# A two-layer hybrid trunk: scan rows loaded two chunks ahead, convolution steps spread over the pieces, output projections in quarters of 512 columns

## The chip, the cores and the metric

The kernel runs on one core of a Trainium2 chip. The metric is the device time of one execution in microseconds (us), the median of several runs. Five engines work side by side and wait for each other by semaphores: PE (TensorE, matrix products into PSUM), DVE (VectorE), ACT (ScalarE), POOL (GpSimd) and SP (SyncE, which here only issues transfers). Each engine takes its instructions in the order that was fixed when the kernel was built.

## The reference, cut to what matters

One sequence of 1024 tokens, width 1024, passes through two residual layers and a final norm.

```
u = rmsnorm(x)                                  # layer 0
z, xBC, dt, q, k, v, g = split(u @ w_in)
xBC = silu(causal_dwconv(xBC))                  # 4 taps; gives xs, B, C
y_a = rmsnorm((ssd_scan(xs, dt, A, B, C) + xs * D) * silu(z))   # 4 groups of 4 heads, chunks of 128
y_b = rmsnorm(diff_attention(q, k, v)) * silu(g)                # 8 heads
x = x + concat(y_a, y_b) @ w_out                # 2048 -> 1024
u = rmsnorm(x)                                  # layer 1
q, f, i, g = split(u @ w_in)
x = x + (rmsnorm(gated_linear_recurrence(q, f, i)) * silu(g)) @ w_out   # 16 heads, 2048 -> 1024
out = rmsnorm(x)
```

## The kernel before, in words

Every large product is made in three passes (hi*hi, hi*lo, lo*hi): each operand is split into a rounded part and a rest. `_wprep` does that for a block of weights of 1024 rows by 256 columns: two transfers into `w_raw` (two buffers), a cast on ACT (L132, `w_hi`) and a subtraction on DVE (L133, `w_lo`). `w_hi` and `w_lo` have two buffers each. `mm_cm` (L174) makes products of 512 columns with the weights stationary, `mm_tm` (L184) products of 256 columns with the activations stationary.

Tiles come from tags with a fixed number of buffers (`SLOTS`); whoever wants a buffer waits until its last user is done. Tags that matter here: `A` (11 buffers of 4 KB a partition), `V` (4), `G` (2), `wT`, `th`, `ey` and `cm` (1 each), `u` (16). PSUM has two banks of tag `pj`, two of `s1` and two double banks `big`. The builder orders the instructions of all engines by its own estimate of times, except PE's in the scan stage of layer 0, where the order is written out by `weave`.

**Start.** `norm_first` loads eight row tiles of x, scales each (L848, by a factor from DVE and POOL), transposes them and splits them into `u`. `setup_rows` loads small rows of parameters, which the first split needs too. The first block of weights is asked for after that.

**Scan stage.** For each of the four groups, `ssd_pieces` makes twelve pieces of 24 products for the next group: four for xs, four for B and C, four for the gate z. After the fourth and the eighth piece all convolution taps (L435) and their SiLU (L438, L439) follow at once. A gate piece leaves PSUM by `silu2`: a Tanh on ACT into `th` (L232), then DVE (L233) into an `A` tile. `weave` puts the scan of the present group between these pieces: `first(c)` of chunk c after piece 1.5 + 1.5c, `second(c)` two pieces later; in the last group, whose pieces are the attention's first ones, after 1.5 + c. `first` loads the rows of cumulated decays for four heads, spread over 128 partitions (`R`, L464), and makes the scores from them (L482, L484, L485). `second` makes the products, loads another spread copy of the decays for every two chunks (`ea`, L523, exponential L525), combines (L529, L530), and for every two chunks adds the skip (L537), gates (L540), squares into `th` (L542) and sums the squares on POOL (L544, L547).

**Output projections.** In both layers `out_proj` walks column blocks of 256. The first half of the contraction (8 tiles of `ya`) runs for both halves of the tokens and is added to x1. The second half (8 tiles of `yb`) has the halves of the tokens outside and the column blocks inside, so its weights are split twice; it ends with the sums of squares (L781) and `finish`: the next layer's norm and transposes, or the final scaling and the store (L998 to L1004). `load_y` brings two tiles at a time through `w_raw`, or one through `th` or `ey`, and splits them.

Of the kernel before, what the change touches and what calls it, by code (L numbers as in the profile page):

```python
# [19 lines left out]
P = 128  # L20
# [69 lines left out]
class Net:  # L90
# [23 lines left out]
    def _wprep(self, i):  # L114
# [4 lines left out]
        hi = self.t("w_hi", [P, KT, WB], F32R)  # L119
        lo = self.t("w_lo", [P, KT, WB], F32R)  # L120
        for q in range(2):
            raw = self.t("w_raw", [P, KT // 2, WB])
            k0 = q * (KT // 2)
            o = 0
            for c0, n in cols:
                nc.sync.dma_start(
                    raw[:, :, o:o + n],
                    src[row0 + k0 * P:row0 + (k0 + KT // 2) * P, c0:c0 + n].rearrange(
                        "(k p) n -> p k n", p=P))
                o += n  # L130
            hq, lq = hi[:, k0:k0 + KT // 2, :], lo[:, k0:k0 + KT // 2, :]
# [47 lines left out]
    def mm_tm(self, out, w, uh, ul, ks=range(KT)):  # L179
        nc = self.nc  # L180
        wh, wl = w
        for k in ks:
            for j, (uu, ww) in enumerate(((uh, wh), (uh, wl), (ul, wh))):
                nc.tensor.matmul(out, lhsT=uu[k], rhs=ww[:, k, :],  # L184
                                 start=(k == 0 and j == 0), stop=(k == KT - 1 and j == 2))
# [20 lines left out]
    def proj_v(self, u):  # L206
        vs = []
        run(self.v_pieces(u, vs))
        return self.v_of(vs)

# [202 lines left out]
def ssd_pieces(S, u, g, out):  # L413

    nc = S.nc

    def conv(w, cis):
        outs = [S.t("A", [P, L]) for _ in range(2)]
        rps = [S.t("V", [P, L]) for _ in range(2)]
        for hf in range(2):  # L420
            for mt in range(2):
# [7 lines left out]
                if not (hf and mt):  # L429
                    yield  # L430
        for mt in range(2):
            cv, rp, ci = outs[mt], rps[mt], cis[mt]
            for k in range(2, -1, -1):
                d = 3 - k
                nc.vector.scalar_tensor_tensor(cv[:, d:], rp[:, :L - d], S.convw[:, k, ci:ci + 1], cv[:, d:],  # L435
                                               op0=ALU.mult, op1=ALU.add)
            th = S.t("p1", [P, L])
            nc.scalar.activation(th, cv, AF.Tanh)  # L438
            nc.vector.scalar_tensor_tensor(cv, th, 1.0, cv, op0=ALU.add, op1=ALU.mult)  # L439
        out.extend(outs)  # L440
        yield

    yield from conv(S.wnext(), (2 * g, 2 * g + 1))
    if g == 0:
        dt_stage(S, u)
    yield from conv(S.wnext(), (8 + g, 12 + g))
    zg = []
    for _ in S.gate_pieces(u, "AA", zg):
        yield
# [3 lines left out]
def ssd_steps(S, g, tiles, ya, at, lag):  # L453
# [4 lines left out]
    X_, sts, eas = {}, {}, {}  # L458

    def first(c):  # L460
        x0, x1, Bt, Ct = tiles[:4]
        cs = slice(c * P, c * P + P)
        R = S.t(("G", "G", "wT")[(8 * g + c) % 3], [P, 4, P])
        nc.sync.dma_start(R, bc(S.acs_d[hs, cs].unsqueeze(0), [P, 4, P]))  # L464
# [15 lines left out]
        nc.vector.tensor_tensor(cb, pt[:, 384:512], S.triu, op=ALU.mult)  # L480
        for h in range(4):
# [4 lines left out]
        X_[c] = pk, R  # L486

    def second(c):
        Ct = tiles[3]
        cs = slice(c * P, c * P + P)  # L490
        pk, sc = X_[c]
# [26 lines left out]
        if c % 2 == 0:  # L518

            c2 = slice(c * P, (c + 2) * P)  # L520
            ea = S.t("ey", [P, 2, 256])
# [4 lines left out]
            eas[c // 2] = ea, S.t("o", [P, 2, 256])  # L526
        ea, tt = (z[:, :, (c % 2) * P:(c % 2) * P + P] for z in eas[c // 2])
# [5 lines left out]
        if c % 2 == 1:  # L533
            t = eas[c // 2][1]
# [6 lines left out]
            sq = S.t("th", [P, 2, 256])  # L541
# [147 lines left out]
def load_y(S, y_d, wcols, hf, k, tags):  # L689

    nc = S.nc
    n = len(tags)
    raw = S.t("w_raw" if n == 2 else (("th", "ey")[k % 2] if hf else "th"), [P, n, 512])
    nc.sync.dma_start(raw, y_d(k, n)[:, :, hf * 512:hf * 512 + 512].rearrange("b p t -> p b t"))
# [500 lines left out]
```

## Time and profile before

| | |
|---|---|
| median of 3 runs | 2238.65 us (2238.03 to 2240.89) |
| profiled execution | 2242.69 us, its span 2240.9 us |
| PE busy | 2178.8 us, 97% of the span |
| DVE, ACT, POOL busy | 1269.9, 832.2, 188.8 us |
| granted clock of TensorE, mean | 0.991 |
| PE in the chain that ended last, L174 and L184 | 24% and 19% |

The span runs from the first to the last instruction of the profiled execution. Busy time is time in which an engine had an instruction at work; PE's matmuls overlap, so its rate is read from the distance of their starts. The granted clock is 1.00 at 2.4 GHz and 0.50 at 1.2 GHz.

### The profile page before, as it was taken

How to read it: one execution, taken by the hardware profiler on the slowest of the kernel's cores; microseconds unless marked ns; L12 is line 12 of the kernel's file. 1: busy time of each engine (PE TensorE's matmuls, PEld its weight loads, DVE VectorE, ACT ScalarE, POOL GpSimd, SP SyncE). 2: the span in 40 equal slices, each digit the busy share in tenths (PEclk: the TensorE clock that was granted, in tenths of full speed). 3: DMA queues.
4: the chain of work that ended last, by engine and by line, in shares of the span. 5: the costliest groups of instructions: out<-in, count | busy, mean ns of one | idle time of the engine just before them, and what ended most of it. 6: DMA issues, size and time to landing. Idle time of an engine off the chain costs nothing.

```text
span 2240.9 us, 40897 instructions
## 1 busy us (share of the span) xinstructions
PE 2178.8 (97%) x16868; PEld 1920.3 (86%) x16868; DVE 1269.9 (57%) x2864; ACT 832.2 (37%) x1903; POOL 188.8 (8%) x216
## 2 busy tenths in 40 slices
PE   6998998899999999999999999999999999999998
PEld 5787776789898988999988989898989898989998
DVE  4765766565656556755453555555555555557444
ACT  4333333234444545644442323232323222324233
POOL 1001111110000000000010010101010101010000
PEclk9999999999999999999999999999999999999999
DMA  4322233332212221525331111111111111125333
GB/s 138 67 84 66 80 85 81 74 81 64 69 36 67 64 69 41 170 66 159 119 104 39 48 48 48 48 48 48 48 48 48 48 49 48 48 67 165 111 103 122
DMA packets 182256, 169.14 MB, mean 75 GB/s; under 512 B 10239, under 2 KB 163233, under 8 KB 182068
## 3 DMA queue, kind: packets, MB, share of 16 engines
q1 hardware_dynamic: 174564, 152.42, 23.1%
q0 software_dynamic: 3280, 9.90, 2.1%
q10 hardware_dynamic: 4224, 4.19, 0.6%
q8 instruction: 132, 2.16, 0.4%
q14 instruction: 56, 0.46, 0.1%
HBM read 132.66 MB, written 25.43 MB: 71 GB/s over the span
## 4 chain that ended last, share of the span: by engine, by line
PE 51%; DMA 1%; ACT 0%; DVE 0%; issue 0%; POOL 0%; POOLq 0%; ACTq 0%
PE pj L174 24%; PE pj L184 14%; PE big L184 5%; PE big L1051 2%; PE big L1139 1%; PE big L1141 1%; PE s L1128 1%; PE big L1093 1%; PE s L1155 1%; PE s L1122 1%; PE big L1087 0%; PE s L159 0%; DMA ey<-yb 0%; DMA th<-in_lvmask 0%; ACT w_hi L132 0%; DVE w_lo L133 0%
## 5 line engine op out<-in xcount | busy, mean ns | idle before, releaser
L174 PE MATMUL pj<-u,w_hi 128*128 128x512 f32 x3072 | 990.0, 400 | 31.3 <-DVE A L233 21.2
L174 PEld LDWEIGHTS pj<-u,w_hi 128*128 128x128 f32 x3072 | 573.4, 190 | 154.7 <-DVE A L233 23.0
L174 PE MATMUL pj<-u,w_lo 128*128 128x512 f32 x1536 | 607.9, 396 | 0.0
L184 PE MATMUL pj<-w_hi,u 128*128 128x256 f32 x2592 | 492.6, 286 | 1.0 <-DVE A L233 1.0
L184 PEld LDWEIGHTS pj<-w_hi,u 128*128 128x128 f32 x2592 | 409.9, 191 | 3.6 <-DVE A L233 1.4
L184 PE MATMUL pj<-w_lo,u 128*128 128x256 f32 x1296 | 368.3, 284 | 0.0
L174 PEld LDWEIGHTS pj<-u,w_lo 128*128 128x128 f32 x1536 | 291.8, 190 | 61.1 <-issue 0.2
L133 DVE TENSOR_TENSOR w_lo<-w_raw,w_hi 128x1024 fp32r<-128x1024 f32 x168 | 206.3, 1251 | 116.9 <-ACT w_hi L132 116.6
L184 PEld LDWEIGHTS pj<-w_lo,u 128*128 128x128 f32 x1296 | 247.8, 191 | 1.0
L132 ACT CAST w_hi<-w_raw 128x1024 fp32r<-128x1024 f32 x168 | 168.1, 1047 | 188.8 <-PE pj L174 107.6
L233 DVE SCALAR_TENSOR_TENSOR A<-th,pj 128x512 f32<-128x512 f32 x80 | 55.1, 689 | 140.9 <-ACT th L232 140.4
L232 ACT ACTIVATE th<-pj 128x512 f32<-128x512 f32 x96 | 57.2, 596 | 208.5 <-PE pj L174 190.8
L617 ACT ACTIVATE p<-p,mx 128x256 f32<-128x256 f32 (+7 forms) x128 | 98.5, 771 | 72.4 <-DVE mx L613 66.4
L148 POOL TENSOR_TENSOR ro<-rs_t,mhalf 128x4 f32<-128x4 f32 x48 | 52.8, 1100 | 682.4 <-DVE rs_t L147 489.1
L603 PE MATMUL big<-A 128*128 128x512 f32 (+3 forms) x384 | 90.3, 352 | 2.6 <-DMA A<-A 1.3
L968 POOL TENSOR_SCALAR A<-th,fN,fB 128x512 f32<-128x512 f32 x32 | 47.6, 1488 | 470.0 <-ACT th L965 470.0
L637 ACT COPY wT<-s 128x512 f32<-128x512 f32 (+2 forms) x96 | 45.8, 477 | 95.8 <-PE s L635 95.1
L639 PE MATMUL s<-V,wT 128*128 128x128 f32 x576 | 79.7, 275 | 0.6 <-ACT wT L637 0.6
L1035 DVE TENSOR_TENSOR A<-A,p 128x512 f32<-128x512 f32 x96 | 65.8, 686 | 23.5 <-PE big L1051 23.0
L639 PEld LDWEIGHTS s<-V,wT 128*128 128x128 f32 x576 | 74.4, 191 | 3.3 <-ACT wT L637 1.1
L1030 DVE TENSOR_TENSOR p<-p,p 128x512 f32<-128x512 f32 x96 | 66.2, 690 | 15.5 <-PE big L1087 6.2
L603 PEld LDWEIGHTS big<-A 128*128 128x128 f32 x384 | 64.5, 189 | 11.3 <-issue 2.3
(330 smaller groups left out, 2977.1 us busy)
## 6 DMA issues: line engine op xcount, KB each, us to landing
w_raw<-in_even_w_in SPq DMA_DIRECT2D x32, 512.0 KB, 4.7
w_raw<-in_odd_w_in SPq DMA_DIRECT2D x64, 256.0 KB, 3.3
w_raw<-in_odd_w_in SPq DMA_DIRECT2D x32, 512.0 KB, 3.9
w_raw<-in_even_w_in SPq DMA_DIRECT2D x48, 256.0 KB, 4.3
w_raw<-in_even_w_out SPq DMA_DIRECT2D x24, 512.0 KB, 4.4
w_raw<-in_odd_w_out SPq DMA_DIRECT2D x24, 512.0 KB, 4.6
A<-A POOLq DMA_DIRECT2D x32, 256.0 KB, 5.5
yo<-ey SPq DMA_DIRECT2D x32, 256.0 KB, 2.0
```

The lines of the kernel that those rows point to most:

```text
L132: nc.scalar.copy(hq, raw)
L133: nc.vector.tensor_tensor(lq, raw, hq.bitcast(F32), op=ALU.subtract)
L148: return nc.gpsimd.tensor_tensor(dst, t[:, :n], self.mhalf[:, :n], op=ALU.pow)
L174: nc.tensor.matmul(out, lhsT=ww[:, k, ms], rhs=uu[k][:, sl], start=(n == 0), stop=(n == 3 * KT - 1))
L184: nc.tensor.matmul(out, lhsT=uu[k], rhs=ww[:, k, :], start=(k == 0 and j == 0), stop=(k == KT - 1 and j == 2))
L232: nc.scalar.activation(th, pj, AF.Tanh, scale=0.5)
L233: nc.vector.scalar_tensor_tensor(out, view(th), 1.0, view(pj), op0=ALU.add, op1=ALU.mult)
L603: nc.tensor.matmul(s[:, k0:k0 + kn], lhsT=q[:, isl], rhs=ks[j][:, k0:k0 + kn], start=(j == 0), stop=(j == 1))
L617: nc.scalar.activation(p[:, :n], p[:, :n], AF.Exp, bias=mx, accum_out=z)
L639: nc.tensor.matmul(po[:, i % 4, :], lhsT=wT[:, j * P:j * P + P], rhs=V(j, hh), start=(j == 0), stop=(j == i))
L1030: nc.vector.tensor_tensor(q, q, bc(t0, [P, L // (2 * h), h]), op=ALU.mult)
L1035: nc.vector.tensor_tensor(k, k, bc(halves(Ts[h], 1)[1], [P, L // (2 * h), h]), op=ALU.mult)
```

## The change

- `rows_load` loads the rows of decays for two chunks at once (256 tokens), into the same three buffers (`G`, `G`, `wT`), when the pair before it begins. `first` takes its 128 columns from there. `ea` is no transfer any more: two exponentials on ACT take it from those rows, into `ey` or `cm`, before DVE changes them in place.
- The squares go into the chunk's own tile `pk` (over X and Xd) and no longer into `th`.
- The convolution's taps and SiLU become single steps in a list; two are taken after every piece.
- In the last group the scan steps stand 1.2 pieces apart and not 1.
- The first block of weights is asked for before `setup_rows`, with its DVE work queued behind the scaling of the fourth row tile.
- `out_proj` takes weights as blocks of 512 rows by 512 columns, two at a time. `sums` goes over pairs of token tiles, 512 columns in one PSUM bank, 12 products for each quarter. Both halves of the contraction go over both halves of the tokens, so the second half's weights are split once. `load_y` loads one tile straight into the second half of its own buffer.
- The final scaling and store are made row tile by row tile in `finish.row`; sums of squares and evictions are 512 columns wide.

```diff
+        wid = sum(n for _, n in cols)
+        kt = KT * WB // wid
+        hi = self.t("w_hi", [P, kt, wid], F32R)
...
+    def rows_load(self, i):
+        if i < 16:
+            g, q = divmod(i, 4)
+            self.rows[i] = self.t(("G", "G", "wT")[i % 3], [P, 4, 256])
+            self.nc.sync.dma_start(self.rows[i], bc(
+                self.acs_d[4 * g:4 * g + 4, q * 256:q * 256 + 256].unsqueeze(0), [P, 4, 256]))
...
+        return [lambda: tap(2), lambda: tap(1), lambda: tap(0), silu]
...
+                if hf:
+                    todo.extend(conv(outs[mt], rps[mt], ci))
+                yield
...
+    for _ in pieces():
+        for _ in range(2):
+            if todo:
+                todo.pop(0)()
         yield
...
     def first(c):
-        R = S.t(("G", "G", "wT")[(8 * g + c) % 3], [P, 4, P])
-        nc.sync.dma_start(R, bc(S.acs_d[hs, cs].unsqueeze(0), [P, 4, P]))
+        if c % 2 == 0:
+            S.rows_load(4 * g + c // 2 + 1)
+        R = S.rows[4 * g + c // 2][:, :, (c % 2) * P:(c % 2) * P + P]
...
+        ea = S.t(("ey", "cm")[c % 2], [P, 2, P])
+        for hh in range(2):
+            nc.scalar.activation(ea[64 * hh:64 * hh + 64], R[64 * hh:64 * hh + 64, hh::2], AF.Exp)
...
     def second(c):
-            for hh in range(2):
-                nc.sync.dma_start(ea[64 * hh:64 * hh + 64],
-                                  bc(S.acs_d[4 * g + hh:4 * g + 4:2, c2].unsqueeze(0), [64, 2, 256]))
-            nc.scalar.activation(ea, ea, AF.Exp)
...
-            sq = S.t("th", [P, 2, 256])
+            sq = pk[:, 0:512].rearrange("p (b t) -> p b t", b=2)
...
 def load_y(S, y_d, wcols, hf, k, tags):
+        y = S.t(tag, [P, 2, 512], F32R)
+        raw = y[:, 1].bitcast(F32)
+        nc.sync.dma_start(raw, y_d(k + j, 1)[0, :, hf * 512:hf * 512 + 512])
...
 def out_proj(S, y_d, wcols, x_d, x1_tags, rs_a, finish):
+    def sums(ws, ys):
+        for t in range(0, NT, 2):
+            pas = [S.ps("pj") for _ in range(2)]
+            order = ((0, 0), (1, 0), (0, 1), (1, 1)) if t in (0, NT - 2) else ((0, 0), (0, 1), (1, 0), (1, 1))
+            for j, kq in order:
+                hf, tt = divmod(t + j, 4)
+                y = ys[hf][4 * kq:4 * kq + 4]
+                S.mm_tm(pas[j], ws[kq], *([z[:, i, tt * P:tt * P + P] for z in y] for i in range(2)),
+                        first=kq == 0, last=kq == 1)
+                if t == NT - 2 and j == 1:
+                    S._wprep(S.wpos + kq)
+                if kq == 1:
+                    yield hf, tt, pas[j]
...
+    for n in range(2):
+        ws = pair()
+        for hf, t, pa in sums(ws, late):
+            if n == 0 and hf == 0:
+                for k in (2 * t, 2 * t + 1):
+                    late[1] += load(1, KT + k, tags1[k])
+            xr = x1s[hf, n, t // 2][:, t % 2]
+            nc.vector.tensor_tensor(xr, pa, xr, op=ALU.add)
...
 def norm_first(S, x, wcol):
-        if hf:
-            S._wprep(0)
...
         if hf == 0:
+            with S.tc.issue_after(scaled.ins):
+                S._wprep(0)
             setup_rows(S)
...
-                steps = ssd_steps(S, g, tiles, ya, lambda c: 1.5 + c, 2)
+                steps = ssd_steps(S, g, tiles, ya, lambda c: 1.5 + 1.2 * c, 2)
```

## Rows read from the trace of the kernel before

**Rows 1.** The page, part 1: busy us, share of the span, instructions.
```profile
PE 2178.8 (97%) x16868; PEld 1920.3 (86%) x16868; DVE 1269.9 (57%) x2864; ACT 832.2 (37%) x1903; POOL 188.8 (8%) x216
```

**Rows 2.** Window of the scan stage: length, busy time of each engine, granted clock, DMA share, GB/s.
```profile
100.00:410.00 310.00, 280.27 (x1393) 225.76 (x1392) 197.98 (x401) 106.06 (x175) 35.55 (x43) 0.95 0.29 77
```

**Rows 3.** Waits of PE over the span: us in total, times, longest.
```profile
PE pj L174 <- DVE A L233: 21.2, 7, 5.6
...
PE pj L174 <- DVE A L570: 8.5, 2, 8.0
...
PE big L184 <- DVE w_lo L133: 1.3, 2, 0.7
...
PE big L184 <- DVE bt L778: 1.2, 1, 1.2
```

**Rows 4.** Timeline from 173 us: start, us, instruction, idle before and releaser.
```profile
174.62 1.44 POOL L544 TENSOR_TENSOR V<-th 128x256 f32<-128x256 f32 x1 [3.83 <-ACT th L542]
...
176.09 0.60 ACT L232 ACTIVATE th<-pj 128x512 f32<-128x512 f32 x1 [1.55 <-POOL V L544]
176.72 0.69 DVE L233 SCALAR_TENSOR_TENSOR A<-th,pj 128x512 f32<-128x512 f32 x1 [0.25 <-ACT th L232]
```

**Rows 5.** Timeline of DVE, ACT and PE from 191 us.
```profile
191.86 0.29 DVE L482 TENSOR_SCALAR wT<-wT,ph 128x128 f32<-128x128 f32 x1 [3.28 <-DMA wT<-acs_d]
...
192.34 0.38 PE L466 MATMUL s<-A 128*128 128x128 f32 x2
...
194.11 0.69 DVE L233 SCALAR_TENSOR_TENSOR A<-th,pj 128x512 f32<-128x512 f32 x1
```

**Rows 6.** Timeline of DVE from 397 us.
```profile
397.62 0.42 DVE L529 TENSOR_TENSOR o<-big,ey 128x256 f32<-128x256 f32 x1 [0.55 <-PE big L508]
...
400.17 0.87 DVE L537 SCALAR_TENSOR_TENSOR o<-A,dcol,o 128x256 f32<-128x256 f32 x2
402.55 0.88 DVE L482 TENSOR_SCALAR wT<-wT,ph 128x128 f32<-128x128 f32 x4 [1.51 <-DMA wT<-acs_d]
...
404.73 1.30 DVE L570 SCALAR_TENSOR_TENSOR A<-pj,A 64x512 fp32r<-64x512 f32 x2
```

**Rows 7.** Waits of DVE and of ACT, 100 to 410 us.
```profile
DVE G L482 <- DMA G<-acs_d: 26.0, 12, 3.3
...
ACT ey L525 <- DMA ey<-acs_d: 42.9, 12, 6.5
```

**Rows 8.** Windows of PE at work at clock 0.50: the first of six, and their sum.
```profile
177.84:181.25 3.41, 3.41 (x10) 2.63 (x9) 0.70 (x4) 0.26 (x1) 0.00 (x0) 0.50 0.15 47
...
sum 23.53, PE 23.52 PEld 18.56 DVE 10.31 ACT 5.78 POOL 4.80; mean PE 3.92 PEld 3.09 DVE 1.72 ACT 0.96 POOL 0.80
```

**Rows 9.** The chain in order of time: start, us, products in an unbroken row.
```profile
1192.19 10.91 PE pj L174 x48
1203.30 5.67 PE pj L174 x24
...
2102.57 48.83 PE pj L184 x407
```

**Rows 10.** Groups of 2029 to 2234 us: weight splits, evictions, small ACT work.
```profile
L133 DVE TENSOR_TENSOR w_lo<-w_raw,w_hi 128x1024 fp32r<-128x1024 f32 x22 | 26.3, 1221 | 4.2 <-ACT w_hi L132 4.2
...
L132 ACT CAST w_hi<-w_raw 128x1024 fp32r<-128x1024 f32 x22 | 22.1, 1045 | 47.2 <-PE big L184 30.4 <-PE pj L184 13.8 <-DMA w_raw<-in_odd_w_out 3.0
...
L781 ACT ACTIVATE cm<-A 128x256 f32<-128x256 f32 x20 | 8.3, 417 | 13.9 <-DVE A L778 13.5
```

**Rows 11.** The page, part 6: DMA issues, count, KB each, median us to landing.
```profile
w_raw<-in_odd_w_out SPq DMA_DIRECT2D x24, 512.0 KB, 4.6
```

**Rows 12.** Timeline of the start.
```profile
13.18 0.54 POOL L148 TENSOR_TENSOR rs<-rs_t,mhalf 128x1 f32<-128x1 f32 x1 [1.96 <-DVE convb L269]
...
15.75 1.23 DVE L133 TENSOR_TENSOR w_lo<-w_raw,w_hi 128x1024 fp32r<-128x1024 f32 x1 [2.45 <-ACT w_hi L132]
...
16.89 0.75 DVE L848 TENSOR_SCALAR A<-A,rs 128x1024 f32<-128x1024 f32 x1
```

More of the change, by code (lines that the diff above doesn't have):

```diff
@@ L176, in mm_cm, with mm_tm @@
                 n += 1
-    def mm_tm(self, out, w, uh, ul, ks=range(KT)):
+    def mm_tm(self, out, w, uh, ul, first=True, last=True):
         nc = self.nc
         wh, wl = w
-        for k in ks:
+        kt = len(uh)
+        for k in range(kt):
             for j, (uu, ww) in enumerate(((uh, wh), (uh, wl), (ul, wh))):
                 nc.tensor.matmul(out, lhsT=uu[k], rhs=ww[:, k, :],
-                                 start=(k == 0 and j == 0), stop=(k == KT - 1 and j == 2))
+                                 start=(first and k == 0 and j == 0), stop=(last and k == kt - 1 and j == 2))
     def v_pieces(self, u, vs):
@@ L428, in conv, with pieces @@
                                      scale=S.convw[:, 3, ci:ci + 1])
[L429 to L440, printed above, removed]
-        yield
[L443 to L449, printed above, removed]
+                if hf:
+                    todo.extend(conv(outs[mt], rps[mt], ci))
+                yield
+    zg = []
+    def pieces():
+        yield from products(S.wnext(), (2 * g, 2 * g + 1))
+        if g == 0:
+            dt_stage(S, u)
+        yield from products(S.wnext(), (8 + g, 12 + g))
+        yield from S.gate_pieces(u, "AA", zg)
+    for _ in pieces():
+        for _ in range(2):
+            if todo:
+                todo.pop(0)()
+        yield
+    assert not todo
     out.append(zg)
@@ new lines, in out_proj @@
+    tags1 = "V", "V", "G", "G", "p0", "p0", "p1", "wT"
+    ss = [S.sm.tile([P, 4, 2], F32, name="ss4", bufs=2) for _ in range(2)]
+    for n in range(2):
+        ws = pair()
+        rss = []
+        for hf, t, pa in sums(ws, late):
[4 more added lines that the diff above has]
+            nc.vector.tensor_tensor(xr, pa, xr, op=ALU.add)
+            jk = S.t("ey", [P, 512])
+            nc.scalar.activation(jk, xr, AF.Square, accum_out=ss[hf][:, t, n:n + 1])
+            if n == 0:
+                finish.early(xr)
+                continue
@@ L795, in out_proj @@
             rss.append(rs)
-        finish(hf, x1s[hf], rss)
+            finish.row(hf, t, [x1s[hf, m, t // 2][:, t % 2] for m in range(2)], rs)
+            if t == 3:
+                finish(hf, x1s, rss)
+                rss = []
 def wspecs(a):
@@ L812, in wspecs @@
             specs.append((W, 0, [(AV0 + (h + 1) * P, WB)]))
[L813 removed]
+    out = lambda w: [(w, kq * 512, [(n * 512, 512)])
+                     for half in (0, 2) for n in range(2) for kq in (half, half + 1)]
     l0 = specs + out(WO)
```

201 lines of the change are left out of this document (81 added, 120 removed).

## Prediction

> **What bounds the kernel now.** I read the page's busy times first. PE works 97% of the span, DVE 57% and ACT 37% [rows 1], so a gain can only come from time in which PE stands still, runs at the low clock, or makes its products in a costlier shape. The windows by stage then say where it stands still: of the 62 us between busy time and span, 29.7 lie between 100 and 410 us, the scan stage, where PE works 280.27 of 310 us at a mean clock of 0.95 [rows 1, 2].
>
> PE's waits name what ends the pauses of the scan stage: seven waits for the gate's DVE step L233 (21.2 us) and two for the attention's split L570 (8.5 us) [rows 3]. The timelines show what stands behind these. At 173 us ACT's Tanh into `th` waits until POOL has summed the squares that lie in the same single buffer; only then can L233 empty the bank that PE wants [rows 4]. At 191 us DVE stands 3.28 us at L482 because the rows of decays have not landed, and L233 comes behind it; the first scan product of chunk 7 is just over then [rows 5]. At 402 us the same L482 stands before L570 [rows 6]. Over the stage, L482's waits for rows in `G` alone are 26.0 us on DVE, and ACT waits 42.9 us for the transferred `ea` [rows 7]. The pauses have a second price: six stretches in which PE is at work again but at clock 0.50, 23.53 us together [rows 8].
>
> In the output projections PE hardly waits: 1.3 us for new weights and 1.2 us for an eviction [rows 3]. There the shape counts. 407 products of 256 columns in an unbroken row took 48.83 us, 0.1200 us each, and 48 of 512 columns took 10.91 us, 0.2273 us each [rows 9].
>
> **The scan stage.** Idle time there is 310 - 280.27 = 29.7 us [rows 2]. Work at half clock would have taken half the time at full, so 23.53 us hold 11.8 us of loss [rows 8]. Together 41.5 us can be won. The squares leave `th`, so the Tanh no longer waits for POOL. The rows are asked for some three pieces before use, about 16 us at 24 x 0.2273 = 5.5 us a piece [rows 9], so L482 does not wait for them either. Three things stay, because the 11 buffers of `A` do not change while two groups together want 12 tiles. First, the last gate tile takes the buffer of B, which is free after chunk 7's first scan product; then L233 must run, 0.69 us, before PE gets its bank [rows 5]. I keep 0.6 us of each of three such pauses: 1.8. Second, the attention's first piece needs a buffer that `second(7)` frees: L529 0.42, another of its size (L530), half of L537's pair 0.44, the ACT split, taken as 0.6 like the Tanh on 512 columns, and half of L570's pair 0.65 follow each other [rows 4, 6], 2.5 us, and 3.2 with one more L570 ahead on DVE. After it a stretch at half clock of the size of the old one, 4.4 us, costs 2.2. Third, 0.6 us of small waits for evictions. That leaves 7.8, and the stage gains 41.5 - 7.8 = 33.7 us. The bounds are 41.5 and, if the long waits only change their cause, about 13.
>
> `ea` costs ACT two more instructions of 64 rows by 256 for every chunk and saves one of 512 columns for two. The nearest rows are 0.42 us for 256 columns [rows 10] and 0.60 for 512 [rows 4]; I take 0.4 each, between nothing and 0.6. Then 32 chunks cost 64 x 0.4 - 16 x 0.60 = 16 us more on ACT, which is busy 106 of 310 us [rows 2]: hidden. It adds a wait, though: L482 now comes after ACT's exponentials, and behind L482 on DVE stand L233 and the convolution's taps, for which PE and ACT wait. With rows that landed long before, ACT can do them early; if it does not, the rival below sets in. The taps in pairs and the spacing of 1.2 move DVE work and add none, on an engine busy 198 of 310 us [rows 2]; I cost them at nothing. SP loses two transfers of `ea` for every two chunks and one of rows, so nothing new is queued there.
>
> **The output projections.** Each layer has 16 x 8 x 4 x 3 = 1536 products of 256 columns and gets 768 of 512. A pair costs 0.2400 now, one wide product 0.2273: 12.7 ns x 768 x 2 layers = 19.5 us. The other rate in the chain, 24 products in 5.67 us, is 0.2363 [rows 9] and would leave 5.7; it holds the end of a row, and the rows here are longer, so I take the first.
>
> The Trainium skill, page "TensorE: Matmul & The Clock Gate", section "Back-to-back issue gap", gives N/2.4 ns plus about 2.5 ns for one product behind another. The trace does not agree: 120.0 and 227.3 ns stand against 109.2 and 215.8. By the page a pair would save only 2.5 ns and the two layers 3.8 us; by the rows they save 19.5.
>
> A new wait can arise where one pair of weight blocks follows another. The first block's buffer is free two quarters before the end, 2 x 12 x 0.2273 = 5.5 us; two casts of 1.05 and one subtraction of 1.22 behind them need 3.3 us [rows 10]. The second block's transfers can only go out as `w_raw` is emptied, 4.6 us [rows 11], then 1.05 + 1.22, about 7 us after the subtraction, and the block is wanted 10.9 us after the first was freed at the earliest. The first block has two us to spare, the second's last half, freed 1.05 us later, about half a us. I count 0.5 us for each of six such places, as the old waits for weights were; they replace 2.5 us of old waits [rows 3], so about nothing net. The four weight blocks fewer in each layer are ACT, DVE and DMA work that PE does not wait for. On SP, 32 loads of one `y` tile take the place of 21 of one or two in each layer, and 16 weight transfers that of 24; none waits for `w_raw` any more, each waits for its own tile's buffer. Eviction of 512 columns takes 0.69 as a 512-column DVE step does [rows 5], against 5.5 us for a tile's products: hidden.
>
> **Start and end.** The fourth row tile's factor is ready at 13.72 us, but DVE takes the weights' subtraction first and scales at 16.89 [rows 12]. With the subtraction behind it, the scaling can begin 3.1 us earlier. The small rows come behind 1 MB of weights now, which may take some of it back. I take 2.5, between 0 and 3.2. At the end the last eviction and square are 512 columns wide: 0.69 + 0.60 in place of 0.42 + 0.42 [rows 4, 10], 0.45 us more, and two scalings become one on ACT, some 0.15 to 0.4 less: 0.3 us lost at most.
>
> **Sum.** 33.7 + 19.5 + 2.5 - 0.3 = 55.4 us off an execution of 2242.69 us. The median is 4.0 us lower, and I take the difference off that: 2183 us. For small waits in the new projections I add one: 2184.
>
> **Rivals.**
> *All of the scan's loss goes.* 7.8 us more: 2176, and with the best of the other bounds 2172. Against it speaks the count of `A` buffers.
> *Long waits of the scan stay under another name.* `second` of an odd chunk now holds `pk` until POOL has summed, and L482 waits for ACT. If two thirds of L233's 21.2 us [rows 3] and half of the 11.8 us of half clock stay, 14 + 6 = 20 us are not won: 2204. For it speaks a DVE at 64%, against it a `pk` that is wanted again only two and a half pieces later.
> *The width hardly counts.* If wide products stand 0.2363 us apart, as in the shorter row [rows 9], 5.7 us are won in place of 19.5: 2198. The unbroken row speaks against it. The Trainium skill's rule above belongs to this case, with 3.8 us won.
> *Slower: the pairs of blocks are prepared one after the other.* If a weight transfer is queued on SP behind a load that waits for its buffer, each of six turnarounds costs two full preparations, 2 x (4.6 + 2 x 1.05 + 1.22) = 15.8, less the 5.5 covered: 10.3 us, 62 together [rows 10, 11]. That gives 2246. It decides from 55 / 6 = 9 us a turnaround. Against it: the first block's raw parts can land long before their turn.
>
> **How the numbers follow.** Forecast 0.70, all goes 0.08, long waits stay 0.12, width 0.05, slower 0.05. The likeliest is 2184; its own range is 2176 to 2198, from the bounds of the start and of the waits for weights. 2172 to 2206 takes in the first four cases and leaves out the slower one and the tails. About 0.2%, 4.5 us, is what a measurement can tell from no change. Only the last case is on the other side, and a point or two lies between: faster 0.93, same 0.02, slower 0.05.
>
> **What would show it.** In the scan stage the waits of L482 and of L232 for transfers and POOL are gone, PE idles under 8 us of some 280, and at most one stretch at clock 0.50 is left, near the first attention pieces. In the projections the products of L184's successor stand 0.227 us apart, with no wait for `w_lo` over 1 us. The fourth row tile is scaled before 15 us, not at 16.89. The prediction is wrong if PE waits for `w_lo` or `w_hi` at each change of n, if the scan's gaps reappear behind `pk` or `ea`, or if wide products stand 0.236 us apart.

## The result, and the profile after

The changed kernel takes 2209.6 us (median of four runs, 2208.95 to 2211.74), the one before, measured beside it, 2239.77 us (four runs, 2238.03 to 2243.48): a ratio of 0.9865, 95% interval 0.9848 to 0.9882. Forecast were 2184 us, and 2172 to 2206 as the range. The direction was right, the gain was 30 us and not 55.

The page of the changed kernel, part 1, against [rows 1], and the window of its scan stage, against [rows 2] (length, busy time of each engine, clock, DMA share, GB/s):

```profile
PE 2156.1 (98%) x15332; PEld 1832.7 (83%) x15332; DVE 1245.9 (56%) x2816; ACT 826.8 (37%) x1863; POOL 193.2 (9%) x216
```

```profile
100.00:384.00 284.00, 271.88 (x1397) 220.03 (x1396) 195.41 (x404) 124.32 (x219) 36.15 (x42) 0.99 0.29 73
```

PE now stands still 12.1 us of 284, where it stood 29.7 of 310. Its waits from 100 to 440 us (in total, times, longest), against [rows 3]:

```profile
PE pj L176 <- DVE A L594: 6.4, 1, 6.4
PE pj L176 <- DVE A L244: 5.2, 4, 3.5
PE pj L176 <- ACT A L454: 0.6, 2, 0.3
```

L176 and L187 are the products of `mm_cm` and `mm_tm` (L174 and L184 before), L244 is the gate's DVE step (L233 before), L594 the attention's split (L570). Of DVE's twelve waits for rows in `G` [rows 7] one is left from 100 to 384 us, the first, and it is for ACT's exponential:

```profile
DVE G L513 <- ACT ey L511: 4.1, 1, 4.1
```

Of the six stretches at half clock [rows 8] the stage keeps one. PE is at work in the last 4.10 us of its 6.83. Two of half its length come later, around the begin of head 6, where the first layer's projection starts; the kernel before had one of that length there, at 887.81 us:

```profile
375.31:382.14 6.83, 4.10 (x10) 3.27 (x11) 3.16 (x7) 2.34 (x4) 1.45 (x2) 0.50 0.15 51
860.00:863.41 3.41, 3.41 (x10) 2.66 (x9) 1.88 (x8) 2.37 (x4) 0.00 (x0) 0.50 0.20 77
887.30:890.71 3.41, 3.41 (x14) 2.93 (x13) 2.35 (x9) 2.57 (x12) 0.00 (x0) 0.50 0.79 217
```

The chain that ended last, in the second layer's projection, gives the wide products' distance, against [rows 9]:

```profile
2086.53 21.83 PE pj L187 x96
...
2120.16 76.21 PE pj L187 x334
```

334 products in 76.21 us are 0.2282 us each. A pair of narrow ones took 0.2400.

Laid side by side by the starts of the same PE work in both traces, the 33.7 us by which the span is shorter (2240.9 to 2207.2) fall as follows. "Head 6" is its first score product (884.2 and 856.6 us), "second layer" the recurrence's first product (1158.8 and 1132.4), and the recurrence ends with the last product of that line (2062.6 and 2037.2).

| stretch | forecast, us won | measured |
|---|---|---|
| start to the scan's first product (118.4 and 120.4) | 2.5 | -2.0 |
| from there to head 6 | 33.7 | 29.5 |
| head 6 to second layer: first output projection | 9.75 | -1.1 |
| recurrence | 0 | -1.0 |
| second output projection | 9.75 | 9.3 |
| after the last product | -0.3 | -1.0 |

The first projection is the largest miss. The wide products are there, but from 856.6 to 1132.4 us PE stands still 10.8 us, where it stood 5.6 in the same stretch before. The window of that stretch, before and then after, and that of 20 us in which the projection stops (its products start at 986.3 us and then not until 1003.4; before, no such break is over 3.2 us long):

```profile
884.20:1158.80 274.60, 269.00 (x2085) 259.14 (x2084) 158.96 (x399) 132.71 (x315) 14.25 (x21) 0.99 0.41 125
```

```profile
856.60:1132.40 275.80, 264.98 (x1319) 219.01 (x1318) 147.00 (x373) 121.35 (x275) 13.84 (x20) 0.99 0.35 107
983.00:1003.00 20.00, 15.88 (x93) 12.51 (x92) 13.71 (x46) 12.14 (x33) 1.01 (x1) 1.00 0.31 97
```

PE's costliest waits in the stretch, before and then after. They are of the attention's products (L603 before, L627, L659 and L663 after) for what the other engines, or a transfer, make for the head:

```profile
PE big L603 <- DMA A<-A: 1.3, 2, 1.0
PE big L603 <- DVE mf L611: 1.3, 2, 0.8
```

```profile
PE s L663 <- ACT wT L661: 2.1, 2, 1.6
PE s L659 <- DVE p L648: 2.0, 2, 1.3
PE big L627 <- DVE mf L635: 1.8, 3, 0.8
```

Counted from one start on PE to the next, with idle time left out, the projection's products take 180.3 us of the stretch where they took 188.2: 7.9 of the forecast 9.75 us are won there. The 5.2 us more of idle time, and 3.3 us more in the attention's own products, take that back.

The timeline of SP tells why it stops there. The residual's last tiles (L777) want buffers of `A`, behind the `late` tiles of the features (L720), and get them only as heads give them back. Until then L781, the DVE step that adds the residual, cannot empty the two PSUM banks, and PE has the last head alone:

```profile
...
999.85 0.80 SPq L720 DMA_DIRECT2D A<-yb  x2
1000.69 0.43 SPq L777 DMA_DIRECT2D A<-in_x  x1
```

### The profile page after: what moved, and what is told of

It is laid out like the page before. It is cut to its first block, busy times and chain, and to the rows that moved or that the text cites. A ratio compares the mean times of both kernels' runs of the same rounds, so it can differ in the third digit from the quotient of the medians.

```text
span 2207.2 us, 37614 instructions
## 1 busy us (share of the span) xinstructions
PE 2156.1 (98%) x15332; PEld 1832.7 (83%) x15332; DVE 1245.9 (56%) x2816; ACT 826.8 (37%) x1863; POOL 193.2 (9%) x216
## 4 chain that ended last, share of the span: by engine, by line
PE 92%; DVE 3%; DMA 3%; ACT 1%; issue 1%; SPq 0%; POOLq 0%; POOL 0%; DVEq 0%; ACTq 0%
PE pj L176 48%; PE pj L187 26%; PE big L627 3%; PE s L663 3%; PE big L1068 2%; PE big L1156 1%; PE s L659 1%; PE big L1158 1%; PE s L1145 1%; PE big L539 1%; PE big L1110 1%; PE s L1172 1%; PE s L161 1%; PE big L533 1%; PE big L536 1%
## 5 line engine op out<-in xcount | busy, mean ns | idle before, releaser
L176 PE MATMUL pj<-u,w_hi 128*128 128x512 f32 x3072 | 984.0, 398 | 14.7 <-DVE A L594 7.1
L176 PEld LDWEIGHTS pj<-u,w_hi 128*128 128x128 f32 x3072 | 569.7, 189 | 136.3 <-issue 8.7
L176 PE MATMUL pj<-u,w_lo 128*128 128x512 f32 x1536 | 605.0, 394 | 0.0
L187 PE MATMUL pj<-w_hi,u 128*128 128x256 f32 (+1 forms) x2112 | 480.0, 316 | 1.8 <-DVE A L244 1.0
L187 PEld LDWEIGHTS pj<-w_hi,u 128*128 128x128 f32 x2112 | 351.2, 191 | 26.0 <-DVE A L244 1.4
L176 PEld LDWEIGHTS pj<-u,w_lo 128*128 128x128 f32 x1536 | 289.9, 189 | 60.0 <-issue 0.2
L187 PE MATMUL pj<-w_lo,u 128*128 128x256 f32 (+1 forms) x1056 | 332.5, 315 | 0.8 <-DVE w_lo L135 0.7
L135 DVE TENSOR_TENSOR w_lo<-w_raw,w_hi 128x1024 fp32r<-128x1024 f32 x152 | 185.7, 1245 | 128.9 <-ACT w_hi L134 128.7
L134 ACT CAST w_hi<-w_raw 128x1024 fp32r<-128x1024 f32 x152 | 152.6, 1048 | 170.6 <-PE pj L176 118.0
L187 PEld LDWEIGHTS pj<-w_lo,u 128*128 128x128 f32 x1056 | 201.5, 191 | 13.3 <-DVE w_lo L135 2.1
L244 DVE SCALAR_TENSOR_TENSOR A<-th,pj 128x512 f32<-128x512 f32 x80 | 55.1, 688 | 138.6 <-ACT th L243 132.2
L243 ACT ACTIVATE th<-pj 128x512 f32<-128x512 f32 x96 | 57.2, 596 | 191.4 <-PE pj L176 191.1
L627 PE MATMUL big<-A 128*128 128x512 f32 (+3 forms) x384 | 90.8, 355 | 2.4 <-DVE mf L635 1.8
L663 PE MATMUL s<-V,wT 128*128 128x128 f32 x576 | 80.2, 277 | 2.7 <-ACT wT L661 2.7
L661 ACT COPY wT<-s 128x512 f32<-128x512 f32 (+2 forms) x96 | 45.9, 478 | 98.1 <-PE s L659 97.3
L663 PEld LDWEIGHTS s<-V,wT 128*128 128x128 f32 x576 | 75.3, 192 | 6.8 <-ACT wT L661 3.8
L433 DVE SCALAR_TENSOR_TENSOR A<-V,convw,A 128x1023 f32<-128x1023 f32 (+2 forms) x48 | 61.5, 1285 | 23.7 <-ACT A L454 23.6
```

Source lines behind the costliest of these rows:

```text
L134: nc.scalar.copy(hq, raw)
L135: nc.vector.tensor_tensor(lq, raw, hq.bitcast(F32), op=ALU.subtract)
L176: nc.tensor.matmul(out, lhsT=ww[:, k, ms], rhs=uu[k][:, sl], start=(n == 0), stop=(n == 3 * KT - 1))
L187: nc.tensor.matmul(out, lhsT=uu[k], rhs=ww[:, k, :], start=(first and k == 0 and j == 0), stop=(last and k == kt - 1 and j == 2))
L243: nc.scalar.activation(th, pj, AF.Tanh, scale=0.5)
L244: nc.vector.scalar_tensor_tensor(out, view(th), 1.0, view(pj), op0=ALU.add, op1=ALU.mult)
```

## The experiments

Ratios are to the kernel before, on the same chip. Code ahead of an edit is the same in several runs, and their traces tell how much a stretch sways by itself: with the changed start, the scan's first product comes at 118.1 to 123.4 us, as a pause at 100 us is 1.7 to 3.9 us long and half clock follows it in some runs (with the start as it was: 118.4, and 116.6 in e4); head 6 to second layer takes 272.3 to 277.7 us in the runs that leave it as it is (275.8 in the changed kernel itself), and once, in e6, 281.9, where a transfer came late, PE waited 2.8 us and 6.83 us at half clock followed.

**The projections by themselves (e4).** The kernel before with the change's weights, `load_y`, `out_proj` and final norm alone.

```diff
+        lo = self.t("w_lo", [P, kt, wid], F32R)
...
+    def sums(ws, ys):
...
+        for t in range(0, NT, 2):
...
```

> The kernel before, with only the new output projections (weights as 512 by 512 blocks, 512 columns, loads in place, row by row end). Theory: the projections bring what the two traces show at their places, minus 1 us in layer 0 and plus 7 in layer 1, 5 to 8 us in all: 2231 to 2234. Rival: the small gain in layer 0 is an accident of where the scan's gains put the last head, and alone the projections bring the forecast 19.5: 2220.

Measured: 2237.04 us, ratio 0.9995 (0.9982 to 1.0007), span 2235.3. The gain is smaller than either expectation has it. Head 6 to second layer took 277.8 us against 274.6, 3.2 us lost, with one wait of 3.0 us for a `G` tile; the second layer's projection won 9.8, and the recurrence and the end lost 1.5 and 1.4. The edit that should win 19.5 us wins nothing that a measurement can tell, and most of what is missing, 9.75 us and the 3.2, is missing in the first layer.

**The residual's tiles first (e1).** The tiles of x for the second column half are allocated and loaded before the `late` ones.

```diff
+                mine = [(hf, t)] if n == 0 else [(i, j) for i in range(2) for j in (0, 2)] if hf == t == 0 else []
+                for i, j in mine:
+                    x1 = x1s[i, n, j // 2] = S.t(next(tags), [P, 2, 512])
...
```

> The changed kernel, with one edit: the four x1 tiles of the second column half are taken and loaded before the first tiles of the second contraction half take A buffers. Theory: in the changed kernel the last two x1 tiles of layer 0 get their A buffers only at 997 and 1001 us, after the last attention head is done with its own, so PE has no projection products between 983 and 1003 us while that head runs alone. With the buffers taken early the projection fills that stretch, the gain of layer 0 rises from minus 1.1 to some plus 8 us, and the time falls from 2209.6 to 2199 to 2203. Rival: PE runs dry there because the head's own chain of DVE and ACT steps is what ends last; then the gap only moves and the time stays within 2 us of 2209.6.

Measured: 2215.62 us, 0.9899 (0.9884 to 0.9914): slower than the change, so my theory fell. The break of 17.1 us is down to 7.7, but head 6 to second layer now takes 283.5 us. The work that fills it is missing later, as cover for the last head: PE stands 4.9 us for a tile for which it waits 0.5 us in the change. PE's waits from 940 to 1130 us, and what follows the longest:

```profile
PE pj L187 <- ACT G L726: 4.9, 1, 4.9
PE pj L187 <- ACT V L726: 1.9, 2, 1.0
```

```profile
1051.17:1058.00 6.83, 5.85 (x14) 4.59 (x15) 1.38 (x2) 2.68 (x8) 0.00 (x0) 0.50 0.11 35
```

**No need of the last head (e7), and more products ahead of it (e8).** Both stand on e1. e7 reads head 6's rows once more where the last head's are due, so that the last head's result is left out; e8 makes the first quarter of four token tiles, in four banks, before the second quarter.

```diff
-    out_proj(S, lambda k, n: (ya if k < 8 else yb)[k % 8:k % 8 + n], S.ssdw, x,
+    out_proj(S, lambda k, n: (ya if k < 8 else yb)[min(k, 14) % 8:min(k, 14) % 8 + n], S.ssdw, x,
```

```diff
+            if four and t == 0:
+                pb = S.ps("big", [P, 1024])
+                pas += [pb[:, 0:512], pb[:, 512:1024]]
+                order = [(j, kq) for kq in range(2) for j in range(4)]
```

> The kernel of the first experiment (x1 buffers early), in which the second half of the contraction reads the tile of head 6 (of heads 6 and 14 in the scheme of layer 1: tile 14) where the last tile is due; the last head is still computed and stored, its result is not used. Theory: in the first experiment PE ran dry between 1040 and 1053 us, because the projection's own products were used up before the last head's last row tile was done at 1047 us, stored, loaded and split. Without that dependency the dry stretch (6.8 us idle and 3.4 us of half clock) goes, layer 0 gains 9 to 10 us against the first experiment, and the time is near 2206. Rival: the products of the second half were held up by buffers (G, V) of the head, not by its result; then the pause at 1047 us stays.

> The kernel of the first experiment, in which the second half's first column half takes the first quarter of the contraction for four token tiles (two in banks of pj, two in big) before the second quarter, which needs the last head. Theory: 2 x 2.7 = 5.4 us more of products lie in front of the wait for the last head; the dry stretch at 1040 to 1053 us shrinks by at least that, with its half clock by up to 9 us, and the time is 2207 to 2210, below the first experiment and about at the changed kernel. Rival: the tiles' eviction and loads bunch up behind it, and nothing is won.

Measured: 2214.18 us, 0.9882 (0.9867 to 0.9897), and 2215.63 us, 0.9893 (0.9879 to 0.9908). Neither gains what it should. In both the pause before a product that wants a `G` tile stays, 4.9 and 5.0 us. So what PE waits for is not the last head's result. That leaves the buffer: `G` holds the last head's gate. e8 does not show that more work ahead is of no use: its products met a pause of 4.7 us for a `V` tile on the way, and they stand ahead of the head's last transposes (L682), right behind which the pause for `G` begins in e1, e7 and e8.

**Held buffer or shared scratch (e13).** Two causes end close together in e1: `G` is given back when the last head's output is made (L709), and the squares' scratch shares the one `ey` buffer with that output, with the `G` tile's cast behind them on ACT. e13 is e1 with that scratch elsewhere.

```diff
-            jk = S.t("ey", [P, 512])
+            jk = S.t("th", [P, 512])
```

> The run with the residual's tiles loaded early (x1 first), and the scratch of the squares in the second half of the features moved from ey to th. In that run's trace ACT stands 6.14 us at the first of these squares until the last head's output has left ey, at 1050.05 us, with the G tile's cast queued behind it; but the G tile's own transfer was issued only at 1048.41 us, when the last head's gate had been read from its G buffer. Theory: the held G buffer is what sets the pause of 4.93 us, so that it stays above 4 us without ey, and the span within 1.5 us of 2213.9 us. Rival: the shared ey and the order on ACT set it: the pause falls to 1.5 us or less, the half-clock stretch behind it goes, and the span falls to 2206 to 2209 us.

Measured: 2218.27 us, 0.9908 (0.9889 to 0.9926). The pause is 4.7 us, as the theory has it; the span of 2216.3 us is 2.4 above e1's and not within 1.5, as a pause of 1.4 us at 1132.9, where the second layer begins, is new. In the chain of waits the pause for `G` now runs through the buffer alone:

```profile
1046.89 0.76 DVE ey L709
...
1047.67 0.32 SPq L710
...
1048.04 2.72 DMA G<-yb
...
1050.84 0.63 ACT G L726
...
1051.51 4.64 PE pj L187 x10
```

L709 reads the gate, the transfer into `G` starts behind it, then the cast, then PE. For the pause, the theory of the held buffer was right.

**Token half outside (e10), and with the residual's tiles first (e9).** In the second half of the features the token half goes outside the column half again, as in the kernel before; the weights are split twice for it.

```diff
-    for n in range(2):
+    for h2, n in ((0, 0), (0, 1), (1, 0), (1, 1)):
...
-        for hf, t, pa in sums(ws, late):
+        for hf, t, pa in sums(ws, late, range(4 * h2, 4 * h2 + 4, 2)):
```

> The changed kernel with two edits in the output projections alone: the residual's tiles of the second column half are allocated and loaded before the late tiles of the first token half (as in the run x1 first), and the second half of the features runs with the token half outside and the column half inside, as the kernel before had it, the weights loaded and split twice for it. Theory: the first-layer projection gained nothing because, with the column half outside, the second token half's eight tiles are wanted 21.8 us after the second half begins, while the last head still holds their V, G and p buffers; with the token half outside they are wanted 43.6 us after it. Then the empty stretch at 1040 to 1052 us with its half-clock 6.8 us goes, the stretch from head 6 to the second layer's first product falls from 275.8 us to 264 to 269 us, and the span to 2196 to 2201 us. Rival: the last head's own chain, with DVE and ACT as the bound, sets the end of this stretch, and the second splitting of the weights adds to both: the pauses move and the stretch stays at 273 us or more, the span 2205 us or more.

> The changed kernel with the second edit of the run before alone: token half outside, column half inside in the second half of the features. Theory: the pause at 983 to 1003 us (residual tiles that wait for an A buffer) stays, and what follows it is spared: head 6 to second layer 269 to 273 us, span 2201 to 2205 us. Rival: the pause at 983 to 1003 us gives cover to the last head, so that this one is as fast as or faster than the one with both edits.

Measured: e9 2205.74 us, 0.9854 (0.9839 to 0.9868); e10 2211.08 us, 0.9877 (0.9862 to 0.9891). Against e1, which differs by the outer loop alone, e9's stretch is 273.3 and not 283.5 us and no wait for `G` or `V` tiles is left:

```profile
PE pj L187 <- ACT A L726: 1.7, 2, 1.4
PE pj L187 <- ACT w_hi L134: 1.2, 2, 0.7
```

So the second token half's tiles, wanted after 21.8 us in the change and after 43.6 here (96 and 192 products at 0.2273 us), were what e1 ran into. Against the change itself the 2.5 us won in the stretch are less than it sways. e10's span was 2209.5, where both theories gave less than that: its start was 3 us late, its stretch 273.7. But e10 still has the break in the projection, 16.9 us from 988 us on, and its stretch is as long as e9's 273.3. So the break for want of `A` buffers, by itself, costs nothing that these traces tell.

**The first gates (e2, e3, e5).** In the change PE stands 3.48 us at 100.49. ACT's timeline shows that the gate's Tanh (L243) comes behind exponentials (L511) that wait for rows of decays:

```profile
100.84 0.85 ACT L511 ACTIVATE ey<-G 64x256 f32<-64x256 f32 x2 [5.03 <-DMA G<-acs_d]
101.72 0.85 ACT L511 ACTIVATE cm<-G 64x256 f32<-64x256 f32 x2
102.60 0.60 ACT L243 ACTIVATE th<-pj 128x512 f32<-128x512 f32 x1
```

e2 loads the first row in two parts and the next ones behind it. e3 asks for the small rows before the first weights. e5 puts the exponentials of the first four chunks behind group 0's last gate.

```diff
+            with self.tc.issue_after(self.last_row.ins) if i else nullcontext():
+                for o in (0, P) if i == 0 else (0,):
...
```

```diff
-            with S.tc.issue_after(scaled.ins):
+            setup_rows(S)
+            with S.tc.issue_after(S.got.ins):
                 S._wprep(0)
-            setup_rows(S)
```

```diff
-        for hh in range(2):
-            nc.scalar.activation(ea[64 * hh:64 * hh + 64], R[64 * hh:64 * hh + 64, hh::2], AF.Exp)
+        with S.tc.issue_after(gate.ins) if g == 0 and c < 4 else nullcontext():
+            for hh in range(2):
+                nc.scalar.activation(ea[64 * hh:64 * hh + 64], R[64 * hh:64 * hh + 64, hh::2], AF.Exp)
```

> The changed kernel, with the first load of decay rows split in two halves of 128 tokens and each further load of rows queued behind the one before it. Theory: the pause of 3.48 us at 100.49 us comes from three row loads of 512 KB that go out together at 92.4 to 93.9 us, the third pair's first; ACT stands at the first exponential until they have landed, with the gate's Tanh behind it. With the first 256 KB alone in front, they land some 3 us earlier, the pause falls under 1 us and the time by about 3 us. Rival: the rows wait for the store of the decays, which lands only at 92.4 us; then the pause stays over 2.5 us.

> The changed kernel, with the small parameter rows loaded and turned into columns before the first block of weights, whose DVE work is queued behind these columns. Theory: in the changed kernel the rows land 2.6 us later (13.7 in place of 11.1 us) and the columns wait on DVE behind two subtractions of weights (13.73 to 16.08 us), which eats the gain from the earlier scaling; with the rows first the first product with weights starts near 17 us in place of 19.1, and the time falls by about 2 us. Rival: the weights then come later and the first products wait for them; the first product starts at 19 us or later and the time does not fall.

> The changed kernel, with the first four chunks' exponentials of the decay rows queued on ACT behind the last gate Tanh of the first group. Theory: splitting the first row load moved the wait on ACT from the first exponential to the next one and the pause before the gate became 4.52 us; what costs is the order on ACT, where exponentials that wait for rows stand in front of the Tanh. With the Tanh in front the pause of 3.48 us at 100.49 us goes and the first scan product comes 2 to 3 us earlier; the time falls by about 3 us to 2206 or 2207. Rival: the gate's DVE step then waits behind the rows' subtractions on DVE instead, and the pause stays over 2.5 us.

Measured: e2 2211.98 us, 0.9880 (0.9866 to 0.9895). The first exponentials run 4 us earlier, the next stand at 101.81 us with the gate still behind them, and PE's pause is 4.5 us: an earlier row does not help as long as the order stands. e3 2214.07 us, 0.9886 (0.9869 to 0.9903): the first product comes at 18.3 and not 19.1 us, but the other runs, which do not have this edit, have it between 18.2 and 19.1. The columns are there at 11.8 us, but a subtraction stands ahead of the fourth row tile's scaling again, at 15.84 us, so e3 moves the wait and does not tell what the order of the columns is worth. e5 2204.96 us, 0.9844 (0.9829 to 0.9858): the pause is gone, the Tanh waits for PE's product only, and the scan begins at 116.8 us:

```profile
100.71 0.60 ACT L243 ACTIVATE th<-pj 128x512 f32<-128x512 f32 x1 [3.28 <-PE pj L176]
```

The two other runs with this edit, e12 and e14, have 116.8 and 116.4, below all runs that have the changed start without it.

**The first attention piece (e6, e11).** PE stands 6.39 us at 371.65 in the change. DVE's timeline there:

```profile
372.15 0.68 DVE L594 SCALAR_TENSOR_TENSOR A<-pj,A 64x512 fp32r<-64x512 f32 x1
...
374.83 0.88 DVE L561 SCALAR_TENSOR_TENSOR o<-A,dcol,o 128x256 f32<-128x256 f32 x2
...
375.82 0.69 DVE L516 TENSOR_TENSOR G<-G,p 128x512 f32<-128x512 f32 x1
376.42 0.76 DVE L564 TENSOR_TENSOR o<-o,A 128x256 f32<-128x256 f32 x2
377.20 1.30 DVE L594 SCALAR_TENSOR_TENSOR A<-pj,A 64x512 fp32r<-64x512 f32 x2
```

Between the first map's splits and the second's lies the last chunk's step: skip (L561), gating (L564), the next chunk's scores. e6 gives one query tile a `V` buffer, so that it need not wait for an `A` one; e11 puts the last chunk's second step one piece earlier in groups 0 to 2.

```diff
-        ts = [S.t("A", [P, L], F32R) for _ in range(2)]
+        ts = [S.t("V" if head0 and mt == 0 and m else "A", [P, L], F32R) for m in range(2)]
```

```diff
-        (at(c) + lag, 2 * c + 1, lambda c=c: second(c)) for c in range(NT)]
+        (at(c) + lag - (c == NT - 1 and g < 3), 2 * c + 1, lambda c=c: second(c)) for c in range(NT)]
```

> The changed kernel, with one of the two query tiles of the first attention head in a free buffer of V and not of A. Theory: the pause of 6.39 us at 371.65 us stands because the second query tile gets its A buffer only from the last scan chunk's skip step, after which the split has its place on DVE; with a free buffer only the first query tile waits, for the chunk's product, and the pause falls to 1 to 2.5 us, the time by 4 to 6 us with the half clock behind it. Rival: the order on DVE alone makes it; then the pause stays over 5 us.

> The changed kernel with the second step of each group's last chunk one piece of projections earlier in groups 0 to 2. Theory: the 6.39 us pause at 371.65 us, at the first attention piece, is order on DVE and ACT: the last chunk of group 2 puts its skip, gating and square between the two halves of the first attention split. One piece earlier they are done before it; the pause falls to 1.5 us or less, the half-clock stretch of 6.83 us behind it (3.4 us lost) goes or halves, and the span falls by 5 to 7 us to 2200 to 2202 us. Rival: the queue on DVE is only moved, the second step now waits in front of the projections' own pieces: the pause shrinks and new ones before 371 us take as much; span 2205 us or more.

Measured: e6 2209.83 us, 0.9861 (0.9844 to 0.9877), the pause 5.12 us: another buffer alone does little, as the rival has it. e11 2199.52 us, 0.9831 (0.9814 to 0.9847). The pause is gone, with the half clock behind it; three waits of 0.5 us for DVE's state update (L546) are new. The scan takes 728.8 us to head 6, the change 736.2. PE's waits from 100 to 440 us:

```profile
PE pj L176 <- DVE A L244: 4.8, 4, 3.1
PE big L533 <- DVE p L546: 1.0, 2, 0.5
PE big L533 <- DVE bt L546: 0.5, 1, 0.5
```

**Together (e12), and once more without the shared scratch (e14).** e12 holds the edits of e1, e5, e9 and e11; e14 adds that of e13.

> The changed kernel with the edits that shortened their own stretch, together: the first four chunks' exponentials behind the last gate of group 0 (gate first), the last chunk's second step of groups 0 to 2 one piece earlier, the token half outside the column half in the second half of the features, and the residual's tiles of the second column half loaded early. Theory: the three pauses have separate causes in separate stretches, so that the savings add: 2196.4 us of span with the earlier second step, less 3.6 us (first products of the scan at 116.8 in place of 120.4 us), less 2.5 us (273.3 in place of 275.8 us from head 6 to the second layer): span 2189 to 2192 us, median 2191 to 2195 us. Rival: they share the queues of ACT and DVE, so that one saving is lost behind the other: span 2195 us or more.

> All four edits that shortened their own stretch together (gate first, earlier second step, token half outside, residual tiles early), and the scratch of the squares in th in place of ey. Theory (held buffers): the ey wait lies beside work there, the span stays within 1.5 us of 2189.8 us. Rival (shared ey): the head 6 to second layer stretch falls from 270.2 us by another 2 to 4 us, the span to 2186 to 2188 us.

Measured: e12 2192.53 us, 0.9795 (0.9779 to 0.9812), span 2189.8, in the range in which the savings add. Its scan stage stands still 3.3 us of 284 at full clock, and head 6 to second layer takes 270.2 us, 4.4 less than before the change:

```profile
100.00:384.00 284.00, 280.75 (x1462) 227.98 (x1462) 198.17 (x406) 126.99 (x224) 37.34 (x44) 1.00 0.27 73
```

e14 2194.34 us, 0.9803 (0.9788 to 0.9818), span 2194.7: not the rival, and 3.4 us of span more than the theory allows for (the times themselves do not tell e14 from e12). The chain of waits shows why: the second layer loads its masks into `th` (L973 casts them), now behind the squares, and on DVE the split (L164) that PE wants stands behind that cast. PE waits 2.5 us for it, and 3.41 us at half clock follow:

```profile
1106.09 3.92 DMA th<-in_lvmask
...
1110.03 0.36 DVE ph L973
1110.39 0.67 DVE u L164
```

So what the shared `ey` costs in e12 stays open. e12 has the lowest time of all and beats both kernels.

## Why the prediction was wrong

**Where the gain comes from was right.** But for the first rows, the long waits of L482 and L232 are gone from the scan, and of its 23.53 us of work at half clock 4.10 are left; the pauses at the last gate tile are 0.56 us three times, forecast 0.6. PE's idle time there, 12.1 us and not under 8, is over by the first attention piece and by the pause at 100.49 us. The rivals that make nothing of the width, or pay 10 us at each change of weights, are out: the second layer won 9.3 us of 9.75 at 0.2282 us a product, and PE's waits for `w_lo` in the first are 0.7 us. By the formula for the isolated gap in the Trainium skill ("TensorE: Matmul & The Clock Gate", "Back-to-back issue gap") one layer would have won 1.9 us, an estimate; the Trainium skill itself sets that formula apart from a stream of weight loads and products, and the measurement decides for the rows.

**Failed: "12.7 ns x 768 x 2 layers", the first layer's half of 9.75 us.** The price of the products was near: 7.9 us of it are in the trace. What failed is that the sum took PE alone to be the bound of this stage, as it is in the second layer, and put PE's idle time at nothing. In the first layer the projection is filler: PE makes its products while the last two heads wait for DVE and ACT. Widening it takes away cover, so PE stands still 10.8 and not 5.6 us, mostly for the heads' own steps. The change of loops also makes the projection's tiles wanted sooner, while the heads hold `A`, `V` and `G`. The new wait was priced at the weights, where 0.7 us came, and not at the heads or at the tiles' buffers. e4 shows the loss without the rest of the change; e1 shortens the break at `A` and uncovers the wait at `G`, e13 shows the cause of that wait, e9 takes it away. No run widens the products and leaves the loads and their order as they were, so how much the width does by itself is not shown. With all of it mended, e12 wins 4.4 of the 9.75 us, one trace against one in a stretch that sways by 5. Part of the rest lies where head 6 begins. The window of its first 33.4 us, of before and then of after:

```profile
884.20:917.60 33.40, 31.29 (x195) 27.81 (x195) 23.47 (x64) 20.40 (x46) 1.60 (x3) 0.95 0.54 149
```

```profile
856.60:890.00 33.40, 28.70 (x136) 23.16 (x135) 25.13 (x58) 22.69 (x46) 1.59 (x3) 0.91 0.71 209
```

PE stands 2.6 us more there (4.7 against 2.1), at a lower clock. The longest of these waits, 1.56 us, is for the head's copy L661, which ACT takes behind splits of the first feature tiles (L723):

```profile
884.22 1.95 ACT u L723 x3
...
886.19 0.59 ACT wT L661
...
886.83 1.67 PE s L663 x8
```

No run tried that by itself; whether it makes the rest stays open.

**Failed: the start, 2.5 us.** The step itself was right: the fourth row tile is scaled at 13.06 us, not 16.89. But the small rows land behind the weights, as the text feared, their copy (L272) comes behind two subtractions (L135), and ACT takes the squares of the fifth row tile (L858), for which it waits, ahead of the split that the first product needs. That product gains 0.4 us:

```profile
13.06 0.75 DVE L861 TENSOR_SCALAR A<-A,rs 128x1024 f32<-128x1024 f32 x1 [0.66 <-POOL rs L150]
...
13.73 2.35 DVE L135 TENSOR_TENSOR w_lo<-w_raw,w_hi 128x1024 fp32r<-128x1024 f32 x2
...
16.00 0.23 DVE L272 COPY cols<-s 128x74 f32<-128x74 f32 x1
...
17.33 1.06 ACT L858 ACTIVATE p<-A 128x1024 f32<-128x1024 f32 x1 [3.62 <-DMA A<-in_x]
```

Then 2.4 us are lost up to the scan's first product, by a wait that the text looked for on DVE and that came on ACT: the exponentials that take the place of a transfer wait for rows, with a gate behind them. "With rows that landed long before" does not hold for the first rows, three loads of 512 KB at once. e5 shows that the order on ACT makes this pause. How much is lost differs from trace to trace, 118.1 to 123.4 us for the same code; even without the pause, at 116.4 to 116.8, the 2.5 us cannot be told from what the start as it was gives, 116.6 and 118.4.

**Mis-sized: the first attention piece, 3.2 us.** It took 6.39. The half clock behind it was sized right: 4.10 us of work, 2.1 lost, forecast 2.2. The steps that follow each other on DVE were the right kind, but the sum ended at the first map's split; the second map's, with the last chunk's skip and gating before it, came on top, and without them in between, in e11, the pause is gone. With these 3.2 us the scan's 33.7 come to 30.5, against 29.5 measured; that stretch also holds the half clock at 860.00 us, a loss of 1.7 that is in no term, so that the two meet in part by luck. One reading was off as well: of the two waits for L570 the second, 0.5 us, is not in the scan stage but at head 6, at 886 us.

**Mis-sized, small:** the tail cost 1.0 and not 0.3 us, and the recurrence 1.0, which was not looked into.

## What to carry to other kernels

Price an edit in the stage in which it lies: where work is filler for something that waits, making it cheaper or earlier may win nothing until that something is shorter, and may hit a buffer that it had been outrunning. When a load is replaced by compute on an engine that works in order, look at what is queued behind it at the first iteration, when nothing has landed yet. And for a change of loop order, list when each tile is now first wanted and who holds its buffer then.

## What the runs showed of the hardware

The first three row loads were issued within 1.5 us. The landing that the trace has of the two into `G` came 8.9 us after its issue; over the loads of this kind in the whole trace the median is 5.0, and a weight transfer of the same size takes 4.6 us [rows 11].

```profile
G<-acs_d SPq DMA_DIRECT2D x2, 512.0 KB, 8.9
```

A pause does not by its length say whether the low clock follows. After the 3.48 us at 100.49 the change went on at 1.00, and so did e1 after 3.60; after 3.38 us at the same place e6 had 6.83 us at 0.50, though the work around it is the same. The change, and then e6:

```profile
103.97:110.80 6.83, 6.83 (x30) 5.67 (x31) 3.23 (x10) 4.67 (x10) 0.00 (x0) 1.00 0.00 0
```

```profile
102.64:109.47 6.83, 5.75 (x14) 4.49 (x15) 4.07 (x13) 4.45 (x9) 0.00 (x0) 0.50 0.00 0
```
